# A two-layer hybrid attention trunk on one core: xT in another place, products of zeros at the start, some low parts of weights on GpSimd, and a rearranged compression input

## The chip, the core and the metric

The kernel runs on one core of a Trainium2 chip. The engines are TensorE (PE: matmuls, with the weight loads in their own row, PEld), VectorE (DVE), ScalarE (ACT), GpSimd (POOL) and SyncE (SP, which issues most transfers). The metric is the device time of one execution in microseconds; lower is better. Times of a kernel are the median of several runs; the profile comes from one further execution.

## What is computed

256 tokens of width 1024 pass through two layers. Every layer is `x += Mixer(RMSNorm(x))`, then `x += SqReLU-MLP(RMSNorm(x))`, with a hidden width of 4096, and a last RMSNorm follows. Everything is float32.

- Layer 0: one input projection feeds two groups of heads. Eight heads are "native sparse attention" with three branches (compressed blocks, selected blocks, a sliding window), merged by sigmoid gates; four heads are differential attention. Their outputs are concatenated and go through one output projection.
- Layer 1: block-sparse attention with 16 heads (MoBA), then its MLP.

Of layer 0 the compression branch matters here. Its keys and values are cut into overlapping blocks of 32 tokens, 16 apart, and each block goes through a small network:

```python
tok = jnp.arange(nc)[:, None] * CMP_STRIDE + jnp.arange(CMP_BLOCK)[None, :]
blk = kv[:, :, tok] + pos
hid = jax.nn.gelu(blk.reshape(b, g, nc, CMP_BLOCK * d) @ w1)
return hid @ w2
```

## The kernel before

**Three products for one.** To keep float32 accuracy every matrix product is three matmuls in the fast 32-bit format: both operands are split into a high part and the rest, and `hi*hi`, `hi*lo` and `lo*hi` are added in PSUM (`mm3`, L552 to L554). So every operand needs two parts. ACT copies the high part (L492 for weights, L537 for activations) and DVE subtracts it from the original to get the low part (L495 for weights, L543 for activations).

**Weights** come from HBM as about 200 pieces of 128 x 1024 (512 KB), in the order of use, through five buffers `raw`. `loads` issues the transfers on SP, `splits` makes the two parts, in six slots: three pairs `whi`/`wlo` in the pool `hot`, and three pairs `vhi`/`vlo` in another. `region` gives a piece a slot of one or the other kind, after how its matmuls use it. A `raw` buffer is free again after the low part is made.

**Activations.** `xT` holds the transposed, normalized input (`xTh`, `xTl`), `mT` the output of the heads. Both lie in `hot`. Late parts of `xT` and `mT` also serve as slots for weights, which is why groups such as `xTl<-raw` appear in the profile.

**Start.** Six matmuls of zeros (L519) run while the first data come. Then for both halves of the tokens: sums of squares on ACT and DVE, `rstd` on POOL (L577, L579), the scaling on DVE (L935, with the norm's weights spread over partitions by L919 on PE), eight transposes per half (L615), the split of the transposed tile (`xTh` on ACT, `xTl` on DVE), and the first projection: 24 matmuls of 280 columns (values and gates, unit "vg") per half. The bias table is made by two matmuls (L731), copied (L735), written to HBM (`ud`) and read back in another shape as `B` (2 MB). Unit "k" and the queries follow.

**Heads.** Logits on PE (L778), bias and maximum on DVE (L788, which needs B), exponential on ACT (L792), scaling by `co` and a gate on DVE and POOL (L849), transposes on PE (L812), the split of the transposed probabilities into `Th` and `Tl` (L537, L543), and the product with the values. Differential heads add L1001, L1014 (`KZ`) and L1264 to L1306.

**Compression input.** `got_ckv` (from L954) takes the projected keys and values from PSUM and writes them in the order that the block network needs into `mT`'s low tile: a high copy `kcv` on ACT (L958), four high parts (two on ACT, L972, two on POOL, L976), and four low parts on DVE (L980).

**Order.** Nothing is ordered at run time. A planner (class `Plan`) simulates the engines while the program is built: each step has an engine, or several to choose from, an estimated duration (`t_act`, `t_dve`) and an urgency. Whenever an engine is free, the ready step with the lowest urgency number is written next. On the chip every engine goes through its instructions strictly in that order.

Of the kernel before, what the change touches and what calls it, by code (L numbers as in the profile page):

```python
# [73 lines left out]
def _blocks(ins):  # L74
# [44 lines left out]
    free = set(range(len(out)))  # L119

    def mlp(l):
# [30 lines left out]
def _lay_out(ins):
    f = {k: np.asarray(ins[k]) for k in ins}
    blocks, still = _blocks(ins)
# [9 lines left out]
    for i, nm in enumerate(("ev_lam_q1", "ev_lam_q2", "ev_lam_k1", "ev_lam_k2")):  # L164
# [158 lines left out]
class Slots:  # L323
# [33 lines left out]
    def serve(self):  # L357
        while self.waiting:
            ev, n, only = self.waiting[0]
            got = [i for i in self.items if only is None or only(i)][:n]  # L360
            if len(got) < n:
                return
            self.waiting.pop(0)
            self.items = [i for i in self.items if not any(i is g for g in got)]
# [10 lines left out]
def trunk_kernel(ctx: ExitStack, tc: tile.TileContext, x, w, prm_d, gs, cst_d, eye, out, widths):  # L375
    nc = tc.nc
    widths, still = zip(*widths)
# [178 lines left out]
    def rstd(t, deps):  # L556
# [397 lines left out]
    def got_ckv(b, evs):  # L954

        kcv = acts.tile([128, 2, S], F32R, name="kcv", tag="scr")
# [4 lines left out]
        out = []  # L961
        for g in range(2):
            r = slice(64 * g, 64 * g + 64)
            for s in range(2):
# [653 lines left out]
```

## Time and profile before

| | us |
|---|---|
| median of 3 runs (636.5 to 640.12) | 638.49 |
| the profiled execution | 636.71 |
| its span, first to last instruction | 634.7 |
| PE busy in the span | 619.5 (98%) |
| DVE busy | 399.5 (63%) |
| ACT busy | 354.3 (56%) |
| POOL busy | 92.3 (15%) |

PE counts as busy from a matmul's start to its modelled end, so 98% means that it hardly ever stood idle, not that it ran at its peak. The granted clock was 0.993 of full on average. Some 2 us of the execution lie outside the span. The share of an engine over the whole span says little about the stage in which another engine waits for it, so the rows below are of single stretches.

### The profile page before, as it was taken

Reading aid. Unit: us, or ns where it says so; the run is one execution under the profiler, and the core shown is the slowest. Engines: PE = TensorE matmul, PEld = TensorE weight load, DVE = VectorE, ACT = ScalarE, POOL = GpSimd, SP = SyncE. Lnnn points to the kernel's source line nnn. Section 1 sums busy time; section 2 is a strip of 40 time slices with the busy share of each in tenths; the row PEclk is TensorE's granted clock in tenths of the full one; section 3 lists DMA queues with packets and bytes.
Section 4 is the critical chain, followed back from the end, with each engine's and each line's share of the span. In section 5 each row is a group of like instructions: output and inputs, shape, how many; then the busy total and the mean of one; then the engine's idle time right before and its main releaser. Section 6 shows DMA issues by size and latency. Waiting matters only on the chain.

```text
span 634.7 us, 10488 instructions
## 1 busy us (share of the span) xinstructions
PE 619.5 (98%) x4022; PEld 562.9 (89%) x4022; DVE 399.5 (63%) x722; ACT 354.3 (56%) x647; POOL 92.3 (15%) x111
## 2 busy tenths in 40 slices
PE   8989999899999999999999999999999999999995
PEld 6989899788889899998988999988889999898994
DVE  6899688958743535444576488895753545445264
ACT  5777478746744536343653488975654535345261
POOL 2022011120111211112110011210021211112011
PEclk7999999999999999999999999999999999999999
DMA  8864423514854564645646343562574564645421
GB/s 329 276 243 149 151 101 103 166 65 138 287 175 164 192 207 158 219 154 193 205 166 206 122 140 132 165 202 67 169 269 161 173 223 149 223 162 192 173 68 66
DMA packets 32100, 109.51 MB, mean 173 GB/s; under 512 B 3361, under 2 KB 5681, under 8 KB 32050
## 3 DMA queue, kind: packets, MB, share of 16 engines
q1 hardware_dynamic: 31186, 106.22, 49.8%
q0 software_dynamic: 576, 2.10, 1.1%
q8 instruction: 31, 0.51, 0.3%
q10 hardware_dynamic: 288, 0.52, 0.2%
q14 instruction: 19, 0.16, 0.1%
HBM read 107.76 MB, written 1.07 MB: 171 GB/s over the span
## 4 chain that ended last, share of the span: by engine, by line
PE 86%; DVE 7%; ACT 2%; issue 2%; DMA 2%; POOL 0%; POOLq 0%; DVEq 0%; ACTq 0%
PE ps L554 27%; PE ps L553 26%; PE ps L552 26%; PE ps L778 2%; DMA raw<-in_w_dram 2%; PE ps L812 1%; DVE wlo L495 1%; PE ps L615 1%; DVE vlo L495 1%; DVE mTl L980 1%; DVE Tl L543 1%; ACT P L792 0%; PE ps L519 0%; DVE x L1335 0%; DVE KZ L1014 0%
## 5 line engine op out<-in xcount | busy, mean ns | idle before, releaser
L495 DVE TENSOR_TENSOR vlo<-raw,vhi 128x1024 fp32r<-128x1024 f32 (+1 forms) x96 | 116.6, 1218 | 130.6 <-ACT vhi L492 130.3
L492 ACT ACTIVATE vhi<-raw 128x1024 fp32r<-128x1024 f32 (+1 forms) x96 | 100.3, 1049 | 157.1 <-PE ps L553 144.7
L552 PE MATMUL ps<-xTh,vhi 128*128 128x256 f32 x640 | 182.1, 285 | 0.0
L554 PE MATMUL ps<-xTh,vlo 128*128 128x256 f32 x640 | 181.1, 283 | 0.0
L553 PE MATMUL ps<-xTl,vhi 128*128 128x256 f32 x640 | 181.0, 283 | 0.0
L553 PEld LDWEIGHTS ps<-xTl,vhi 128*128 128x128 f32 x640 | 122.5, 191 | 1.2
L552 PEld LDWEIGHTS ps<-xTh,vhi 128*128 128x128 f32 x640 | 122.5, 191 | 1.2
L554 PEld LDWEIGHTS ps<-xTh,vlo 128*128 128x128 f32 x640 | 122.4, 191 | 0.0
L1398 POOL TENSOR_TENSOR P<-P 128x512 f32<-128x512 f32 x32 | 48.7, 1522 | 308.9 <-ACT P L1395 308.9
L495 DVE TENSOR_TENSOR wlo<-raw,whi 128x1024 fp32r<-128x1024 f32 (+1 forms) x65 | 77.6, 1209 | 9.6 <-ACT whi L492 9.5
L492 ACT ACTIVATE whi<-raw 128x1024 fp32r<-128x1024 f32 (+1 forms) x65 | 66.5, 1040 | 8.9 <-PE ps L554 7.2
L792 ACT ACTIVATE P<-P,nm 128x128 f32<-128x128 f32 x80 | 35.5, 447 | 8.6 <-DVE nm L788 8.5
L552 PE MATMUL ps<-whi,Th 128*128 128x512 f32 x100 | 39.0, 390 | 0.0
L553 PE MATMUL ps<-wlo,Th 128*128 128x512 f32 x100 | 39.0, 390 | 0.0
L554 PE MATMUL ps<-whi,Tl 128*128 128x512 f32 x100 | 38.9, 389 | 0.0
L495 DVE TENSOR_TENSOR mTl<-raw,mTh 128x1024 fp32r<-128x1024 f32 x30 | 35.9, 1219 | 0.1
L492 ACT ACTIVATE mTh<-raw 128x1024 fp32r<-128x1024 f32 x30 | 30.6, 1047 | 1.3 <-PE ps L554 1.3
L1400 DVE TENSOR_TENSOR Tl<-P,Th 128x512 fp32r<-128x512 f32 x22 | 15.2, 693 | 24.9 <-POOL P L1398 24.9
L1395 ACT ACTIVATE P<-ps 128x512 f32<-128x512 f32 x32 | 19.1, 597 | 15.9 <-PE ps L554 12.0
L788 DVE CUSTOM_DVE_ANT_0 P<-ps,B 128x128 f32<-128x128 f32 x80 | 24.5, 351 | 3.7 <-PE ps L778 3.5
L552 PE MATMUL ps<-mTh,Th 128*128 128x512 f32 x68 | 26.6, 391 | 0.0
L553 PE MATMUL ps<-mTl,Th 128*128 128x512 f32 x68 | 26.5, 390 | 0.0
(251 smaller groups left out, 1249.9 us busy)
## 6 DMA issues: line engine op xcount, KB each, us to landing
raw<-in_w_dram SPq DMA_DIRECT2D x192, 512.0 KB, 4.2
B<-ud SPq DMA_DIRECT2D x1, 2048.0 KB, 10.8
gB<-in_gs_dram POOLq DMA_DIRECT2D x4, 512.0 KB, 4.6
x<-in_x_dram SPq DMA_DIRECT2D x2, 512.0 KB, 4.6
raw<-in_w_dram SPq DMA_DIRECT2D x2, 420.0 KB, 5.5
out_dram<-P SPq DMA_DIRECT2D x2, 256.0 KB, 2.1
out_dram<-P ACTq DMA_DIRECT2D x2, 256.0 KB, 2.5
cst<-in_cst_dram SPq DMA_DIRECT2D x1, 372.0 KB
```

The source lines that it names most:

```text
L492: nc.scalar.activation(pc.hi[:, :n], raw[:, :n], AF.Copy)
L495: nc.vector.tensor_tensor(pc.lo[:, :n], raw[:, :n], pc.hi[:, :n].bitcast(F32), OP.subtract)
L543: nc.vector.tensor_tensor(lo, src, hi.bitcast(F32), OP.subtract)
L552: nc.tensor.matmul(out_, ah, bh, start=start, stop=False)
L553: nc.tensor.matmul(out_, ah, bl, start=False, stop=False)
L554: nc.tensor.matmul(out_, al, bh, start=False, stop=stop)
L778: nc.tensor.matmul(ps[:, 128 * qt:128 * qt + nk], q[:, par, ts], k[i][:, par, :nk], start=i == 0, stop=i == 1)
L788: nc.vector.tensor_tensor_reduce(P[:, c], ps[:, c], B[:, h, 0:nk][:, ::-1], -1.0, 3e38, OP.add, OP.min, nm[:, qt:qt + 1])
L792: nc.scalar.activation(P[:, c], P[:, c], AF.Exp, bias=nm[:, qt:qt + 1], scale=-1.0, accum_out=sums[:, qt:qt + 1])
L1395: e = act(t_act(512), lambda: nc.scalar.activation(r, b.t, AF.Relu), got, *deps)
L1398: g = pool(1.225, lambda: nc.gpsimd.tensor_tensor(sq, r, r, OP.mult), e)
L1400: h = dve(t_dve(512), lambda: nc.vector.tensor_tensor(hl, sq, hh.bitcast(F32), OP.subtract), f, g)
```

## The change

- **Places.** All six pairs of weight slots lie in `hot`, in plain order of release; the rule of regions is gone. `xT` moves to the pool `acts`.
- **Products of zeros.** Two further coroutines (`keep_on`) put matmuls of zeros (512 columns, into the bank `ps1`) into PE's order wherever the planner has nothing else for PE, until four pieces of weights have been used. 23 of them come about, besides the six of before.
- **Low parts on GpSimd.** For pieces before number 35 that are at least two ahead of the piece in use, the planner may give the low part to POOL. It does so 14 times.
- **Compression input.** `kcv` holds both parts: ACT makes the high one, DVE the low one, in one 512-wide instruction each, from PSUM. Eight copies then rearrange them into `mT`'s low tile, three on POOL and five on ACT.
- **An estimate.** The planner counts 0.55 in place of 0.93 us for the power in the first norms.

```diff
...
-NEAR = 3
 RAWS, PARTS, NP, URGENT, TAIL, AHEAD = 5, 6, 5, 3, 3, 3
 SECOND, ROOM, LATER = 5, (4, 5), (0, 0.05)
-WARM, WRITE = 6, -1.5
+WARM, WRITE, KEEP, EARLY, SPARE = 6, -1.5, 4, 35, 2
...
-    near = list(zip(tiles(NEAR, [128, 1024], F32R, "whi", hot), tiles(NEAR, [128, 1024], F32R, "wlo", hot)))
+    parts = Slots(plan, list(zip(tiles(PARTS, [128, 1024], F32R, "whi", hot), tiles(PARTS, [128, 1024], F32R, "wlo", hot))))
     tbuf = Slots(plan, list(zip(tiles(2, [128, 512], F32R, "Th", hot), tiles(2, [128, 512], F32R, "Tl", hot))))
-    xT = (hot.tile([128, KT, S], F32R, name="xTh"), hot.tile([128, KT, S], F32R, name="xTl"))
     mT = (hot.tile([128, KT, S], F32R, name="mTh"), hot.tile([128, KT, S], F32R, name="mTl"))
...
-    far = list(zip(tiles(PARTS - NEAR, [128, 1024], F32R, "vhi"), tiles(PARTS - NEAR, [128, 1024], F32R, "vlo")))
-    parts = Slots(plan, [i for p in zip(near, far) for i in p] + near[len(far):] + far[len(near):])
+    xT = (acts.tile([128, KT, S], F32R, name="xTh"), acts.tile([128, KT, S], F32R, name="xTl"))
...
-            got = pc.slots.get(only=region(p) if pc.slots is parts else None)
+            got = pc.slots.get()
...
-            def lo(pc=pc, raw=raw, n=n):
-                nc.vector.tensor_tensor(pc.lo[:, :n], raw[:, :n], pc.hi[:, :n].bitcast(F32), OP.subtract)
+            def lo(eng, pc=pc, raw=raw, n=n):
+                eng.tensor_tensor(pc.lo[:, :n], raw[:, :n], pc.hi[:, :n].bitcast(F32), OP.subtract)
 
             e = act(t_act(n, False), hi, got, loaded[p], u=urgency)
-            f = dve(t_dve(n), lo, e, u=urgency)
+            ways = [(DVE, t_dve(n), lambda lo=lo: lo(nc.vector))]
+            if p < EARLY and p - Piece.current >= SPARE:
+                ways.append((POOL, 0.1 + n / 320, lambda lo=lo: lo(nc.gpsimd)))
+            f = plan.step(ways, [e], urgency)
...
+    def keep_on(z):
+
+        yield zero_e
+        while Piece.uses < KEEP:
+            yield pe(0.23, lambda: nc.tensor.matmul(banks[1].t, z[:, :128], z, start=True, stop=True), u=9)
+
+    for _ in range(2):
+        plan.spawn(keep_on(tbuf.items[1][0]))
...
-        whole = act(t_act(512), lambda: nc.scalar.activation(kcv, ps, AF.Copy), *evs, bank=b)
+        ev = split_out(kcv[:, 0], kcv[:, 1], ps, 512, evs, bank=b)
+        bank_a.put(b, [ev[1]])
...
+        for h in range(2):
+            for g in range(2):
+                for s in range(2):
+                    o, t = slice(64 * s, 64 * s + 64), slice(16 * s, 16 * s + 240)
+                    dst = ckv[o, h, :, g, :, 0:15]
+                    src = kcv[64 * g:64 * g + 64, h, :, t].rearrange("p k (c i) -> p k i c", i=16).bitcast(F32)
+                    ways = [(ACT, 0.575, lambda dst=dst, src=src: nc.scalar.activation(dst, src, AF.Copy))]
+                    if g == s:
+                        ways.append((POOL, 1.25, lambda dst=dst, src=src: nc.gpsimd.tensor_copy(dst, src)))
+                    done.append(plan.step(ways, [ev[h]], 1))
...
```

The line numbers move: L552 to L554 become L547 to L549, L495 becomes L478, L543 L538, L615 L610, L731 L726, L788 L783, L849 L844, L812 L807, L919 L914, L1014 L992; the new matmuls of zeros are L511.

**The order at three places.** First, PE at the start, from its first matmul to the first projection. Before (`gB` is the row of the norm's weights, `ident` the unit matrix of the transposes):

```order
L519 MATMUL ps_117<-Th_81 128x512 x6
L919 MATMUL ps_112<-gB,P_99 128x512
L919 MATMUL ps_113<-gB,P_99 128x512
L615 MATMUL ps_114<-ident,P_95 128x128 x4
L615 MATMUL ps_115<-ident,P_96 128x128 x4
L552 MATMUL ps_110<-whi_74,xTh 128x280
L553 MATMUL ps_110<-wlo_77,xTh 128x280
L554 MATMUL ps_110<-whi_74,xTl 128x280
```

And after the change:

```order
L505 MATMUL ps_117<-Th_87 128x512 x6
L511 MATMUL ps_111<-Th_87 128x512 x5
L914 MATMUL ps_112<-gB,P_103 128x512
L914 MATMUL ps_113<-gB,P_103 128x512
L511 MATMUL ps_111<-Th_87 128x512 x5
L610 MATMUL ps_114<-ident,P_99 128x128 x4
L511 MATMUL ps_111<-Th_87 128x512 x2
L610 MATMUL ps_115<-ident,P_100 128x128 x4
L511 MATMUL ps_111<-Th_87 128x512 x8
L547 MATMUL ps_110<-whi_74,xTh 128x280
L548 MATMUL ps_110<-wlo_80,xTh 128x280
L549 MATMUL ps_110<-whi_74,xTl 128x280
```

Twenty zeros stand ahead of the first projection (L547) now, beside the six of before (L505); three more follow between its parts.

DVE's next rows of the start, before, from the first `xTl` on:

```order
L543 TENSOR_TENSOR xTl<-ps_114,xTh 128x4x128
L543 TENSOR_TENSOR xTl<-ps_115,xTh 128x4x128
L495 TENSOR_TENSOR vlo_103<-raw_91,vhi_100 128x840
L935 SCALAR_TENSOR_TENSOR P_97<-x_119,rs,ps_112 128x512
L935 SCALAR_TENSOR_TENSOR P_98<-x_119,rs,ps_113 128x512
L495 TENSOR_TENSOR wlo_78<-raw_92,whi_75 128x560
L495 TENSOR_TENSOR vlo_104<-raw_93,vhi_101 128x1024
L543 TENSOR_TENSOR xTl<-ps_116,xTh 128x4x128
L543 TENSOR_TENSOR xTl<-ps_117,xTh 128x4x128
```

And after:

```order
L538 TENSOR_TENSOR xTl<-ps_114,xTh 128x4x128
L538 TENSOR_TENSOR xTl<-ps_115,xTh 128x4x128
L478 TENSOR_TENSOR wlo_81<-raw_95,whi_75 128x840
L930 SCALAR_TENSOR_TENSOR P_101<-x_119,rs,ps_112 128x512
L930 SCALAR_TENSOR_TENSOR P_102<-x_119,rs,ps_113 128x512
L478 TENSOR_TENSOR wlo_83<-raw_97,whi_77 128x1024
L478 TENSOR_TENSOR wlo_84<-raw_98,whi_78 128x1024
L538 TENSOR_TENSOR xTl<-ps_116,xTh 128x4x128
L538 TENSOR_TENSOR xTl<-ps_117,xTh 128x4x128
```

Ahead of the second half's `xTl` (from `ps_116` and `ps_117`) stood a split of 560 columns and one of 1024; now it is two of 1024, `wlo_83` and `wlo_84`, both used only after the second half.

Second, the compression input in the middle of the first heads, on DVE, before:

```order
L788 ISA nm 128x1
L495 TENSOR_TENSOR vlo_103<-raw_93,vhi_100 128x1024
L842 RECIPROCAL co<-sums 128x2
L849 TENSOR_SCALAR P_97<-P_97,co,gates 128x128
L980 TENSOR_TENSOR mTl<-ps_110,kcv 64x2x16x15 x4
L543 TENSOR_TENSOR Tl_83<-ps_116,Th_81 128x384
L543 TENSOR_TENSOR Tl_82<-ps_117,Th_80 128x384
```

And after (`kcv` is written from itself because both its parts lie in one tile):

```order
L783 ISA P_103,nm<-ps_115,B 128x128
L783 ISA nm 128x1
L538 TENSOR_TENSOR Tl_89<-ps_116,Th_87 128x384
L538 TENSOR_TENSOR kcv<-ps_110,kcv 128x512
L538 TENSOR_TENSOR Tl_88<-ps_117,Th_86 128x384
L837 RECIPROCAL co<-sums 128x2
L844 TENSOR_SCALAR P_102<-P_102,co,gates 128x128
```

The first `Tl` stands ahead of the one instruction on `kcv`, where it stood behind four on `mTl`. POOL around the same place, before:

```order
L849 TENSOR_SCALAR P_95<-P_95,co,gates 128x256
L849 TENSOR_SCALAR P_96<-P_96,co,gates 128x256
L976 CAST mTl<-kcv 64x2x16x15 x2
L849 TENSOR_SCALAR P_97<-P_97,co,gates 128x256
L849 TENSOR_SCALAR P_98<-P_98,co,gates 128x256
```

And after:

```order
L478 TENSOR_TENSOR wlo_82<-raw_96,whi_76 128x560
L478 TENSOR_TENSOR wlo_81<-raw_96,whi_75 128x1024
L478 TENSOR_TENSOR wlo_84<-raw_94,whi_78 128x1024
L478 TENSOR_TENSOR wlo_80<-raw_97,whi_74 128x1024
L478 TENSOR_TENSOR wlo_81<-raw_96,whi_75 128x1024
L965 CAST mTl<-kcv 64x2x16x15 x3
L844 TENSOR_SCALAR P_103<-P_103,co,gates 128x256
L844 TENSOR_SCALAR P_99<-P_99,co,gates 128x128
L844 TENSOR_SCALAR P_100<-P_100,co,gates 128x256
```

Five splits of weights and the three copies now stand ahead of POOL's first scaling of P (L844). SP between the pieces of weights and B, before:

```order
L423 DMA raw_94<-in_w_dram 128x1024
L423 DMA raw_90<-in_w_dram 128x1024
L423 DMA ud<-P_99 16x383
L423 DMA raw_91<-in_w_dram 128x1024
L423 DMA raw_92<-in_w_dram 128x1024
L423 DMA B<-ud 128x16x256
```

And after:

```order
L409 DMA raw_98<-in_w_dram 128x1024
L409 DMA raw_94<-in_w_dram 128x1024
L409 DMA raw_95<-in_w_dram 128x1024
L409 DMA ud<-P_103 16x383
L409 DMA raw_97<-in_w_dram 128x1024
L409 DMA raw_96<-in_w_dram 128x1024
L409 DMA B<-ud 128x16x256
```

One more piece stands ahead of `ud`, and so of B.

Third, DVE near the end of the differential heads, where the slots of `xT` are filled with weights, before:

```order
L1306 TENSOR_SCALAR od_137<-od_137,dr 128x128
L1001 SCALAR_TENSOR_TENSOR QD_107<-ps_110,QD_107 64x256 x2
L1014 TENSOR_TENSOR KZ<-ps_110,KD_109 64x256
L495 TENSOR_TENSOR xTl<-raw_91,xTh 128x1024
L495 TENSOR_TENSOR xTl<-raw_92,xTh 128x1024
L1014 TENSOR_TENSOR KZ<-ps_110,KD_109 64x256
```

And after:

```order
L1278 COPY od_138<-ps_115 128x256
L979 SCALAR_TENSOR_TENSOR QD_107<-ps_110,QD_107 64x256 x2
L992 TENSOR_TENSOR KZ<-ps_110,KD_109 64x256
L540 SCALAR_TENSOR_TENSOR mTl<-ps_116,sub_128,mTh 128x256
L992 TENSOR_TENSOR KZ<-ps_110,KD_109 64x256
L478 TENSOR_TENSOR xTl<-raw_96,xTh 128x1024
```

Both KZ stand ahead of the one `xTl` that DVE has left; the other is on POOL.

## Rows read from the trace of the kernel before

**Rows 1.** Stretches: length, busy time (count) by engine, PE clock, DMA share, GB/s
```profile
0.00:10.00 10.00, 7.67 (x21) 4.30 (x22) 5.29 (x10) 5.40 (x10) 4.48 (x16) 0.92 0.80 283
10.00:20.00 10.00, 10.00 (x58) 9.56 (x58) 8.94 (x18) 7.88 (x15) 0.01 (x1) 0.74 0.92 349
20.00:40.00 20.00, 20.00 (x170) 20.00 (x169) 16.90 (x46) 13.78 (x34) 0.68 (x2) 1.00 0.93 324
40.00:60.00 20.00, 18.02 (x154) 17.68 (x152) 19.61 (x47) 17.50 (x43) 6.16 (x9) 1.00 0.31 103
...
160.00:360.00 200.00, 200.00 (x1233) 180.35 (x1232) 104.41 (x110) 93.30 (x119) 29.33 (x23) 1.00 0.56 188
```

The busy times stand in the order PE, PEld, DVE, ACT, POOL.

**Rows 2.** PE's waits, 16 to 160 us: waited for, total, times, longest
```profile
PE ps L552 <- DVE KZ L1014: 2.7, 1, 2.7
PE ps L553 <- DVE Tl L543: 2.0, 1, 2.0
PE ps L1216 <- DVE cmpb L1208: 0.6, 1, 0.6
PE ps L812 <- POOL P L849: 0.4, 1, 0.4
```

**Rows 3.** Timeline of DVE: start, us, instruction, count [idle before and releaser]
```profile
16.10 0.69 DVE L543 TENSOR_TENSOR xTl<-ps,xTh 128x512 fp32r<-128x512 f32 x1 [0.79 <-ACT xTh L537]
...
41.75 0.87 DVE L849 TENSOR_SCALAR P<-P,co,gates 128x128 f32<-128x128 f32 x1
42.54 3.99 DVE L980 TENSOR_TENSOR mTl<-ps,kcv 64x480 fp32r<-64x480 f32 x4
46.56 1.02 DVE L543 TENSOR_TENSOR Tl<-ps,Th 128x384 fp32r<-128x384 f32 x2
...
59.82 1.22 DVE L495 TENSOR_TENSOR wlo<-raw,whi 128x1024 fp32r<-128x1024 f32 x1
...
119.64 2.34 DVE L495 TENSOR_TENSOR xTl<-raw,xTh 128x1024 fp32r<-128x1024 f32 x2
```

**Rows 4.** Timeline of POOL
```profile
41.13 2.50 POOL L976 CAST mTl<-kcv 64x480 fp32r<-64x480 f32 x2 [0.56 <-ACT kcv L958]
...
47.83 1.17 POOL L849 TENSOR_SCALAR P<-P,co,gates 128x256 f32<-128x256 f32 x2 [3.54 <-DVE co L842]
...
59.72 1.66 POOL L849 TENSOR_SCALAR P<-P,co,gates 128x256 f32<-128x256 f32 x1 [6.58 <-DVE co L842]
...
164.29 1.04 POOL L1398 TENSOR_TENSOR P<-P 128x512 f32<-128x512 f32 x1 [26.25 <-ACT P L1395]
```

**Rows 5.** Timeline of PE at the start
```profile
4.30 2.31 PE L919 MATMUL ps<-gB,P 1*128 1x512 f32 x4
...
9.70 0.60 PE L554 MATMUL ps<-whi,xTl 128*128 128x280 f32 x1 [0.70 <-DVE xTl L543]
...
15.16 0.41 PE L552 MATMUL ps<-whi,xTh 128*128 128x280 f32 x1
15.40 0.30 PE L553 MATMUL ps<-wlo,xTh 128*128 128x280 f32 x1
15.54 0.30 PE L554 MATMUL ps<-whi,xTl 128*128 128x280 f32 x1
...
19.84 0.28 PE L552 MATMUL ps<-xTh,vhi 128*128 128x256 f32 x1
```

**Rows 6.** Timeline of PE in the output projection, two neighbours of 512 columns
```profile
118.92 0.40 PE L552 MATMUL ps<-whi,mTh 128*128 128x512 f32 x1
119.15 0.39 PE L553 MATMUL ps<-wlo,mTh 128*128 128x512 f32 x1
```

**Rows 7.** The page's groups (count, busy, mean ns, idle before) and a DMA issue
```profile
L495 DVE TENSOR_TENSOR vlo<-raw,vhi 128x1024 fp32r<-128x1024 f32 (+1 forms) x96 | 116.6, 1218 | 130.6 <-ACT vhi L492 130.3
...
L495 DVE TENSOR_TENSOR wlo<-raw,whi 128x1024 fp32r<-128x1024 f32 (+1 forms) x65 | 77.6, 1209 | 9.6 <-ACT whi L492 9.5
...
B<-ud SPq DMA_DIRECT2D x1, 2048.0 KB, 10.8
```

More of the change, by code (lines that the diff above doesn't have):

```diff
@@ L118, in _blocks @@
     out += [r(wo, i) for i in range(4)]
-    free = set(range(len(out)))
     def mlp(l):
@@ L138, in _blocks @@
         out.append(t(odd, span(128 * j, 128 * j + 128), span(1024 + 128 * j, 1152 + 128 * j)))
-    free |= set(range(len(out), len(out) + 4))
     out += [r(f["od_w_out"][0], i) for i in range(4)]
     mlp(1)
-    cut, still = [], []
-    for i, b in enumerate(out):
-        stationary = None if i in free else b.ndim == 4
+    cut = []
+    for b in out:
         b = np.ascontiguousarray(b).reshape(128, -1)
@@ L147, in _blocks @@
         cut += [np.ascontiguousarray(c) for c in np.split(b, k, 1)]
-        still += [stationary] * k
-    return cut, still
+    return cut
 def _lay_out(ins):
     f = {k: np.asarray(ins[k]) for k in ins}
-    blocks, still = _blocks(ins)
+    blocks = _blocks(ins)
     prm = np.zeros((128, P_N), np.float32)
@@ L167, in _lay_out @@
     return {"x": np.ascontiguousarray(f["x"].reshape(S, D)), "w": np.concatenate([b.reshape(-1) for b in blocks]),
-            "prm": prm, "gs": gs, "cst": _constants(), "eye": np.eye(128, dtype=np.float32)}, [(b.shape[1], s) for b, s in zip(blocks, still)]
-NEAR = 3
+            "prm": prm, "gs": gs, "cst": _constants(), "eye": np.eye(128, dtype=np.float32)}, [b.shape[1] for b in blocks]
 RAWS, PARTS, NP, URGENT, TAIL, AHEAD = 5, 6, 5, 3, 3, 3
 SECOND, ROOM, LATER = 5, (4, 5), (0, 0.05)
-WARM, WRITE = 6, -1.5
+WARM, WRITE, KEEP, EARLY, SPARE = 6, -1.5, 4, 35, 2
 ORDER = ["vg", "k", "q0", "c", "q1", "h", "dv", "d0", "d1", "d2", "d3"]
@@ L327, in __init__, with get @@
         self.plan, self.items, self.waiting, self.wanted = plan, list(items), [], []
-    def get(self, n=1, only=None):
+    def get(self, n=1):
         ev = Event()
-        self.waiting.append((ev, n, only))
+        self.waiting.append((ev, n))
         self.serve()
@@ L357, in serve @@
     def serve(self):
[L358 to L364, printed above, removed]
+        while self.waiting and len(self.items) >= self.waiting[0][1]:
+            ev, n = self.waiting.pop(0)
+            got, self.items = self.items[:n], self.items[n:]
             self.plan.fire(ev, "slot", got if n > 1 else got[0])
@@ L472, in loads @@
             plan.when([ev], None, lambda p=p, raw=got.value: plan.fire(loaded[p], SP, raw))
-    def region(p):
-        return None if still[p] is None else lambda it: any(it is f for f in far) == still[p]
     def splits():
@@ L578, in rstd @@
             ms = both
-        return rs, pool(0.93, lambda: nc.gpsimd.tensor_tensor(rs, ms, half[:, 0:1], OP.pow), e, half_e, u=-4)
+        return rs, pool(pow_t, lambda: nc.gpsimd.tensor_tensor(rs, ms, half[:, 0:1], OP.pow), e, half_e, u=-4)
     def rvar(t, deps):
@@ L960, in got_ckv @@
         done = split_out(ckv[:, 0, :, :, :, 15], ckv[:, 1, :, :, :, 15], pos, 64, [prm_e])
[L961 to L964, printed above, removed]
-                o, t = slice(64 * s, 64 * s + 64), slice(16 * s, 16 * s + 240)
-                def part(h, src, r=r, o=o, t=t, g=g):
-                    return ckv[o, h, :, g, :, 0:15], src[r, :, t].rearrange("p k (c i) -> p k i c", i=16)
-                def hi(part=part):
-                    dst, src = part(0, ps)
-                    nc.scalar.activation(dst, src, AF.Copy)
-                def same(part=part):
-                    dst, src = part(0, kcv)
-                    nc.gpsimd.tensor_copy(dst, src.bitcast(F32))
-                def lo(part=part):
-                    (dst, src), (_, high) = part(1, ps), part(1, kcv)
-                    nc.vector.tensor_tensor(dst, src, high.bitcast(F32), OP.subtract)
-                if g == s:
-                    done.append(pool(0.9, same, whole))
-                else:
-                    out.append(act(t_act(480), hi, *evs, bank=b))
-                out.append(dve(t_dve(480), lo, whole, bank=b))
@@ L987, in got_ckv @@
-        bank_a.put(b, [whole, *out])
-        done += out
+        for h in range(2):
[8 more added lines that the diff above has]
+                    done.append(plan.step(ways, [ev[h]], 1))
```

12 lines of the change are left out of this document (5 added, 7 removed).

## The prediction, made before the kernel ran

> **What bounds the kernel now.** First I read the table by stretches [rows 1]: what matters there is how full TensorE (PE) is against the other engines and which clock it was granted. From 160 to 360 us PE is busy 200.00 of 200 us; VectorE (DVE) has 104.41. Nothing that the change does to DVE, ScalarE (ACT) or GpSimd (POOL) can shorten that stretch. The same holds for most of what follows, so I look for gains and losses before 160 us only. [...] And from 20 to 60 us DVE is nearly full, 16.90 and 19.61 of 20 us, so whatever PE needs from DVE there comes when DVE's order allows it.
>
> Then the list of PE's waits, 16 to 160 us [rows 2]: four that matter, 2.7 us for KZ from DVE, 2.0 for Tl from DVE, 0.6 for cmpb from DVE and 0.4 for P from POOL, 5.7 us together. That is all the waiting time an edit could give back after the start; the rest of PE's time is matmuls that the change leaves as they are.
>
> **The wait for Tl.** DVE's timeline [rows 3] shows why it is there: four L980 instructions (low parts of the compression inputs) take 3.99 us from 42.54, and only then, at 46.56, comes Tl, for which PE stands. The change puts the low part of the compression input into one instruction from PSUM, with the first Tl ahead of it in DVE's order, and gives the eight copies to ACT and POOL. A 512-wide instruction of this kind costs 0.69 us (L543 at 16.10 [rows 3]), so DVE drops some 3.3 us and PE's 2.0 us go. Bounds: 0 (Tl late for another reason) to 2.0; I take 2.0, since what was ahead of Tl is gone.
>
> **The wait for KZ.** Two L495 splits of the next xT (2.34 us from 119.64 [rows 3]) stand between two KZ instructions; the second KZ frees the bank that PE waits for. After the change both KZ stand ahead of the one xTl split that DVE keeps, and the other goes to POOL. Bounds 0 to 2.7; I take 2.7.
>
> **The small waits.** POOL's P at 59.72 took 1.66 us, where two of the same width took 1.17 together [rows 4]: a DVE split that began at 59.82 [rows 3] stood in its way. Here fewer DVE splits help, but POOL's own splits now stand in the same queue ahead of L844 (L849 before). Bounds −1.0 (both waits gone) to +1.0 (both doubled); I take −0.4.
>
> **The start.** PE's timeline [rows 5] gives the prices. [...] The price of a zero matmul is 0.23 us at the high clock (512 columns, 118.92 to 119.15 [rows 6]); 23 of them are 5.3 us. They stand ahead of first-pass work in PE's order: five ahead of L914 (which ran at 4.30 [rows 5]), five ahead of the first transposes, two between the transposes, eight ahead of the first projection. Walking through with the durations of the timeline: warm-ups to 4.2, zeros to 5.7, L914 some 1.6 (its 2.31 us were partly at the low clock) to 7.3, zeros to 8.4, transposes and two zeros to 9.8, eight zeros to 11.6; 24 matmuls by 0.14 with eight transposes and three zeros end near 16.2; the 24 of the second token half near 19.4; the bias matmuls 0.4, so the first matmul of unit k stands at about 19.8. Before it stood at 19.84 [rows 5]. But the second half needs xTl from DVE. Its last quarter came at 16.10 [rows 3]. In DVE's order two weight splits of 1.21 us [rows 7] stand ahead of it now, one of them in the place of a 560-wide one, which goes to POOL; that is half a microsecond more, and if POOL's split meets one of the two, another 0.5 to 1. So DVE may hold PE until 20.5. I take 0 for the start. Bounds: −2.8 (all of the clock's gain kept) to +2.5 (all the zeros on the path, less the clock's gain).
>
> [...]
>
> **GpSimd's splits.** Thirteen splits of 1024 and one of 560 leave DVE: 13 x 1.21 + 0.73 = 16.5 us off it (1.209 us each [rows 7]; 0.73 taken in proportion with the fixed part). POOL does 512 elements with two inputs in 1.04 us [rows 4], so 1024 take some 2.1 and all fourteen about 28 us. What they cost beyond that is blocking: L849 of POOL took 1.66 in place of 0.58 us [rows 4], and a DVE L849 that met the POOL copy begun at 41.13 [rows 4] took 0.87 us at 41.75 [rows 3], although it works on half the columns. So a meeting costs the later one 0.5 to 1.1 us. If half of the fourteen meet such a DVE instruction, that is 7 x 0.8 = 5.6 us of lateness, less than what DVE is relieved of, but it comes at other places. POOL's own L844 and the copies of the compression input now wait behind splits, too. I book +1.9 us of new waits on PE, a third of those 5.6; bounds 0 to 5.6.
>
> [...]
>
> **The bias transfer.** B, 2 MB, took 10.8 us to land [rows 7] and gates the first heads' softmax. In the queue of SP one more weight piece now stands ahead of it, in front of ud, and of the two behind ud one has a buffer that a POOL split frees. 512 KB at 324 GB/s [rows 1] are 1.6 us. Half of it had cover (DVE had a split to finish before the first head); I take +0.7, bounds 0 to 1.6.
>
> **The layout, and the plain order of the slots.** Pieces of weights lie in two regions already, whi/wlo and vhi/vlo, and the low splits into both take the same time, 1.209 and 1.218 us [rows 7]. So I book 0 for moving tiles; unseen is xT at its new place, a matmul operand of some 2600 instructions: 1 ns on each would be 2.6 us, in either direction. That goes into the range, with a small chance.
>
> **The sum.** −2.0 −2.7 −0.4 +0 +1.9 +0.7 = −2.5 us. The profiled execution took 636.71 us, its span 634.7; so the same execution would take 634.2. It stands 1.8 below the median of the runs shown, 638.49, and what is compared are medians: 638.5 − 2.5 = 636.0.
>
> **Rivals.** (a) *The start gains.* The clock stays up, the zeros end sooner than in my walk, and DVE has xTl ready when PE arrives: −2.8 more, 633.2. For it speaks that half of the 24 + 24 products ran at the low clock; against it that eight zeros stand right ahead of the first product, and that xTl moves back in time on DVE. 22%.
> (b) *GpSimd holds DVE up* in the full stretch from 20 to 60 us: of each pair of instructions that read two operands from SBUF the later stands still. With 19.61 of 20 us taken, DVE has nowhere to catch up, so the 5.6 us show in full and the Tl wait comes back: 638.5 − 2.7 − 0.4 + 5.6 + 0.7 = 641.7, and up to 643 where the POOL queue delays P as well. It decides as soon as more than half of the splits before 60 us meet a DVE split. For it: the 1.66 and 0.87 us; against: 16.5 us are off DVE. 20%. [...]
> (c) *The zeros do not do what they are for.* They shift the first product to 11.6 us and the clock falls anyway while PE stands for xTl: the 24 products keep 0.23 us each, and the start ends some 2 us later: 638.0. 12%.
> (d) My forecast, 634.5 to 637.5: 46%.
>
> **How the numbers follow.** About 0.5%, 3.2 us, is what a measurement of this kernel can tell from no change; faster means below 635.3, slower above 641.7. Faster: (a) 0.22 and the low third of (d), 0.15, together 0.37. Slower: most of (b), and a small part for xT at its new place, together 0.18. The rest, 0.45, within. The range reaches from 631.5 ((a) with the small waits gone) to 642.5 ((b) but for its end). The predicted time is that of (d).
>
> **What would show it.** In the profile after, PE's waits before 160 us: no wait for Tl near 45 and none for KZ near 119. The clock of the first 20 us at or near full from 5 us on, and the first matmul of unit k within a microsecond of 19.8; earlier by two says (a), later by two with a low clock says (c). POOL's splits near 2.1 us where DVE leaves them alone, and longer ones, or DVE splits above 1.6 us, in 20 to 60 us: many of them with PE's waits behind them say (b). The first softmax instruction of the heads near 36 to 37.5. Wrong as a whole I would be if the stretch from 160 us on changed its length by more than 1 us, since I let it alone.

## The result, and the profile after

The changed kernel takes 649.54 us (median of 4 runs, 648.91 to 651.04), the kernel before 639.31 us beside it; the ratio is 1.0158, with an interval of 1.0118 to 1.0198. The kernel became 10 us slower. The prediction, 636.0 with a range of 631.5 to 642.5, was wrong in sign and in range. The nearest case was rival (b), GpSimd holding DVE up; its price of 641.7 was too low.

The profiled execution took 650.0 us, its span 648.1, against 634.7 before. The first transposes of layer 0's MLP, which start at 157.19 us before, start at 168.00: 10.8 of the 13.4 us are lost before that point, 2.6 after it. Up to 1.7 of the 10.8 are the clock's: in this execution its granted share was 0.50 from 132.43 to 135.84 us, behind a wait of PE of 1.8 us, and in the profiled execution of before it stayed at 1.00 in that stretch.

From the page of the changed kernel: busy time (share of the span) and count per engine, two of the costliest groups (count, busy, mean ns, idle before) and the issue of B.

```profile
PE 626.6 (97%) x4045; PEld 564.8 (87%) x4045; DVE 403.9 (62%) x714; ACT 364.4 (56%) x650; POOL 109.4 (17%) x117
...
L478 DVE TENSOR_TENSOR wlo<-raw,whi 128x1024 fp32r<-128x1024 f32 (+1 forms) x144 | 181.0, 1266 | 74.2 <-ACT whi L475 73.8
...
L478 POOL TENSOR_TENSOR wlo<-raw,whi 128x1024 fp32r<-128x1024 f32 (+1 forms) x13 | 30.9, 2378 | 48.7 <-ACT whi L475 39.7
...
B<-ud SPq DMA_DIRECT2D x1, 2048.0 KB, 12.0
```

DVE was relieved of 14 splits and is busy 4 us longer than before: the time that it stands still inside an instruction counts as busy (12.7 us, below), and seven more scalings of P have come to it (L844, 38 in place of 31). POOL's mean of 2378 ns takes in the one split of 560 columns; those of 1024 took 2.35 to 2.73 us, with a median of 2.39.

The stretches that answer to [rows 1], in the same columns:

```profile
0.00:10.00 10.00, 8.56 (x23) 5.63 (x24) 3.59 (x7) 3.11 (x5) 3.76 (x14) 0.98 0.80 271
10.00:20.00 10.00, 10.00 (x60) 9.08 (x59) 8.34 (x15) 7.28 (x14) 2.44 (x3) 0.85 0.81 302
20.00:40.00 20.00, 19.66 (x162) 18.97 (x160) 14.85 (x28) 14.26 (x28) 8.08 (x4) 1.00 0.88 297
40.00:60.00 20.00, 17.38 (x141) 16.50 (x142) 15.48 (x61) 17.84 (x47) 7.50 (x9) 1.00 0.24 90
```

The granted clock rose from 0.92 and 0.74 to 0.98 and 0.85 in the first two stretches, and DVE has idle time again from 40 to 60 us. Both are what the change can be seen to aim at, and neither shows in the time.

PE's waits, 16 to 175 us, for [rows 2]:

```profile
PE ps L773 <- DVE nm L783: 2.2, 1, 2.2
PE ps L547 <- DVE KZ L992: 1.8, 1, 1.8
PE ps L1194 <- DVE cmpb L1186: 1.7, 1, 1.7
PE ps L807 <- DVE P L1254: 1.1, 2, 0.7
PE ps L548 <- DVE Tl L538: 1.1, 3, 0.5
PE ps L1294 <- DVE od L1284: 0.8, 1, 0.8
```

The 2.0 us for one Tl are gone (four short ones are left, none above 0.5), the wait for cmpb has trebled, KZ is still waited for, and there is a new wait of 2.2 us for the first softmax.

DVE's timeline shows what is behind those for cmpb, P and od:

```profile
23.98 1.91 DVE L1028 TENSOR_SCALAR gates<-gates 128x24 f32<-128x24 f32 x1
...
33.68 2.58 DVE L478 TENSOR_TENSOR wlo<-raw,whi 128x1024 fp32r<-128x1024 f32 x1 [0.17 <-ACT whi L475]
...
82.66 1.29 DVE L1179 TENSOR_TENSOR cmpb<-cmpb,mx 128x256 f32<-128x256 f32 x1
...
120.47 2.18 DVE L1243 TENSOR_TENSOR dco<-dco,lam 128x2 f32<-128x2 f32 x1
...
135.15 3.41 DVE L478 TENSOR_TENSOR wlo<-raw,whi 128x1024 fp32r<-128x1024 f32 x1
```

Beside each of them stands a split on POOL; three of the five:

```profile
23.12 2.73 POOL L478 TENSOR_TENSOR wlo<-raw,whi 128x1024 fp32r<-128x1024 f32 x1 [7.17 <-ACT gates L1024]
...
120.25 2.38 POOL L478 TENSOR_TENSOR wlo<-raw,whi 128x1024 fp32r<-128x1024 f32 x1 [6.01 <-ACT whi L475]
...
134.94 2.54 POOL L478 TENSOR_TENSOR wlo<-raw,whi 128x1024 fp32r<-128x1024 f32 x1 [0.60 <-ACT whi L475]
```

An instruction on two numbers per partition (L1243) takes 2.18 us in place of 0.16, because POOL began its split 0.2 us earlier. Nine of the fourteen splits stop a DVE instruction so, by 0.8 to 2.2 us each, 12.7 us in all (each duration less that of the same instruction undisturbed). Only two of the nine lie between 20 and 60 us.

### The profile page after: what moved, and what is told of

Same layout as the page of the kernel before. It is cut to its first block, busy times and chain, and to the rows that moved or that the text cites. A ratio compares the mean times of both kernels' runs of the same rounds, so it can differ in the third digit from the quotient of the medians.

```text
span 648.1 us, 10579 instructions
## 1 busy us (share of the span) xinstructions
PE 626.6 (97%) x4045; PEld 564.8 (87%) x4045; DVE 403.9 (62%) x714; ACT 364.4 (56%) x650; POOL 109.4 (17%) x117
## 4 chain that ended last, share of the span: by engine, by line
PE 78%; DVE 11%; ACT 5%; issue 3%; DMA 2%; POOL 0%; POOLq 0%; SPq 0%; DVEq 0%; ACTq 0%
PE ps L548 24%; PE ps L549 24%; PE ps L547 24%; DVE wlo L478 3%; DMA B<-ud 2%; DVE P L783 1%; ACT P L787 1%; PE ps L511 1%; PE ps L610 1%; PE ps L773 1%; PE ps L807 1%; DVE Tl L538 1%; ACT mTl L963 1%; DVE P L844 1%; ACT Th L532 1%
## 5 line engine op out<-in xcount | busy, mean ns | idle before, releaser
L478 DVE TENSOR_TENSOR wlo<-raw,whi 128x1024 fp32r<-128x1024 f32 (+1 forms) x144 | 181.0, 1266 | 74.2 <-ACT whi L475 73.8
L475 ACT ACTIVATE whi<-raw 128x1024 fp32r<-128x1024 f32 (+1 forms) x157 | 162.9, 1051 | 95.3 <-PE ps L549 65.8
L547 PE MATMUL ps<-xTh,whi 128*128 128x256 f32 x592 | 169.6, 286 | 0.0
L549 PE MATMUL ps<-xTh,wlo 128*128 128x256 f32 x592 | 166.3, 281 | 0.0
L548 PE MATMUL ps<-xTl,whi 128*128 128x256 f32 x592 | 166.2, 281 | 0.0
L547 PEld LDWEIGHTS ps<-xTh,whi 128*128 128x128 f32 x592 | 111.6, 188 | 0.9 <-issue 0.3
L548 PEld LDWEIGHTS ps<-xTl,whi 128*128 128x128 f32 x592 | 111.7, 189 | 0.6
L549 PEld LDWEIGHTS ps<-xTh,wlo 128*128 128x128 f32 x592 | 111.5, 188 | 0.0
L478 DVE TENSOR_TENSOR mTl<-raw,mTh 128x1024 fp32r<-128x1024 f32 x34 | 41.5, 1224 | 22.9 <-ACT mTh L475 22.9
L549 PE MATMUL ps<-whi,Tl 128*128 128x512 f32 x120 | 46.9, 390 | 0.0
L547 PE MATMUL ps<-whi,Th 128*128 128x512 f32 x120 | 46.7, 390 | 0.0
L478 POOL TENSOR_TENSOR wlo<-raw,whi 128x1024 fp32r<-128x1024 f32 (+1 forms) x13 | 30.9, 2378 | 48.7 <-ACT whi L475 39.7
L547 PE MATMUL ps<-xTh,mTh 128*128 128x256 f32 (+1 forms) x128 | 38.4, 300 | 0.0
L548 PE MATMUL ps<-xTl,mTh 128*128 128x256 f32 (+1 forms) x128 | 38.0, 297 | 0.3 <-DVE xTl L478 0.3
L549 PE MATMUL ps<-xTh,mTl 128*128 128x256 f32 (+1 forms) x128 | 37.8, 295 | 0.0
L547 PE MATMUL ps<-whi,xTh 128*128 128x512 f32 (+1 forms) x88 | 34.0, 387 | 0.1
```

The source lines that it names most:

```text
L475: nc.scalar.activation(pc.hi[:, :n], raw[:, :n], AF.Copy)
L478: eng.tensor_tensor(pc.lo[:, :n], raw[:, :n], pc.hi[:, :n].bitcast(F32), OP.subtract)
L547: nc.tensor.matmul(out_, ah, bh, start=start, stop=False)
L548: nc.tensor.matmul(out_, ah, bl, start=False, stop=False)
L549: nc.tensor.matmul(out_, al, bh, start=False, stop=stop)
```

## Experiments

Each kernel was run beside the kernel before, whose medians lay between 639.0 and 640.8 us; times are medians.

**1. Zeros and GpSimd's splits, each taken away.** The diffs to the changed kernel are one line: `KEEP` 4 to 0 (`a_nozero`), `EARLY` 35 to 0 (`a_nopool`), or both (`a_neither`, shown).

```diff
-WARM, WRITE, KEEP, EARLY, SPARE = 6, -1.5, 4, 35, 2
+WARM, WRITE, KEEP, EARLY, SPARE = 6, -1.5, 0, 0, 2
```

Without zeros, nothing but the zeros leaves PE's order; the other engines' orders are the same (but for two DVE instructions of under 0.2 us that change places in the pair without splits). So the four kernels are a square in which zeros are added or taken away alone. Without splits on GpSimd the planner orders the engines anew, so what the splits cost takes in the order that they bring.

> The changed kernel without its 23 products of zeros (the six of before stay); the order of every other instruction on every engine is the changed kernel's. Theory Z (the zeros stand in the way at the start, and what starts late there comes late again at the bias transfer): the first projection starts 3 us or more earlier than at 14.3 us, the bias matmuls near 19 in place of 22.2, the wait for the first heads' bias shrinks, and the time falls by 3 to 5 us to 644.5 to 646.5. [...] Rival P (GpSimd's splits are all of it): within 1 us of 649.5.

> The changed kernel with all low parts of weights on DVE; zeros, layout and compression input stay. Theory P (a split takes GpSimd 2.4 us, in which DVE instructions stand still, short ones too, and buffers come free late): the time falls by 5 to 8 us, to 641.5 to 644.5, and DVE shows no short instruction of over 1 us. Rival: DVE needed the relief, the 16 us of splits are back on it and the time stays above 648.

> The changed kernel without zeros and without splits on GpSimd: layout, slots in plain order and the compression input are left. Theory Z and P together: nothing of the loss is left, 636 to 639. Rival L (the other order that the plain slots bring, or the places, cost most): 643 or above.

Measured: `a_nozero` 648.14 (ratio to before 1.013, 1.0082 to 1.0178), `a_nopool` 640.68 (1.0007, 0.998 to 1.0034), `a_neither` 640.06 (1.000, 0.9973 to 1.0028). The splits on GpSimd account for the loss: without them the kernel is as fast as before, with them it is 8 to 9 us slower, with or without zeros. That is more than theory P gave. The zeros' share came out at 0.6 and 1.4 us, below theory Z, although in the profiles the bias matmuls stand 3 us later. So the square was run again, with more rounds:

> The changed kernel itself, beside the one without zeros, to set a price on the zeros. In the profiles the bias matmuls stand 3.0 to 3.2 us later with zeros (22.2 against 19.0, 21.7 against 18.6), the medians so far differ by 0.6 and 1.4. Theory Z: 2.5 to 4 us above the one without zeros. Rival (the clock gives most of it back later, or other executions start differently than the profiled ones): 0 to 1.5 us above it.

> The changed kernel without its zeros, every other instruction in the same order. Theory Z: 645 to 647, 2.5 to 4 us under the changed kernel beside it. Rival: less than 1.5 us under it.

> Zeros, but no splits on GpSimd. Theory Z: 2.5 to 4 us above the one with neither. Rival: within 1.5 us of it. In both theories 7 to 10 us under the changed kernel, since the splits are taken away.

> Neither zeros nor splits on GpSimd, the same order on all engines as the one with zeros alone. Theory Z: 2.5 to 4 us under that one. Rival: within 1.5 us of it. In both theories before's time within 1.5 us.

Measured: 650.84 and 647.46 with splits, 641.78 (1.0029, 1.0005 to 1.0054) and 638.02 (0.9981, 0.9956 to 1.0006) without. Zeros: 3.4 and 3.8 us this time; the medians of the four pairs together say that they cost, some 1 to 4 us, no closer. Splits: 9.1 and 9.4 us. `z_neither` lies 2.3 us under before, where at most 1.5 was expected.

The traces of the eight executions say more. The first transposes of layer 0's MLP come 4.1 to 5.0 us later with zeros in all four pairs, where both executions of a pair have the clock low equally long between 20 us and that point. Why the medians show less stays open. With splits they come 7.5 to 8.2 us later. In the pair without zeros, `a_nozero` and `a_neither`, this can be taken apart: 163.33 against 155.71 us, 7.6 us. PE's waits from 16 us to there add up to 8.7 against 3.0 us, and the granted clock of `a_nozero` fell to 0.50 for 3.4 us, worth at most half of that (columns as in [rows 1]):

```profile
127.58:130.99 3.41, 3.41 (x13) 3.02 (x12) 3.27 (x8) 2.63 (x6) 2.64 (x5) 0.50 0.46 136
```

That is 5.7 us of waits and up to 1.7 us of clock. In each of the four traces with splits the clock falls once or twice between 20 us and the MLP (to 0.50 for 3.41 us in the changed kernel and in `a_nozero`, twice as long in `z_all`), in none of the four without. Splits are not needed for it: it falls there in `b_xT`, too, from 122.79 to 133.03 us, which has none.

How the zeros stand in the way is seen in PE's timeline of the changed kernel:

```profile
4.17 2.22 PE L511 MATMUL ps<-Th 128*128 128x512 f32 x5
6.32 1.98 PE L914 MATMUL ps<-gB,P 1*128 1x512 f32 x4
...
11.86 2.61 PE L511 MATMUL ps<-Th 128*128 128x512 f32 x8
14.30 0.29 PE L547 MATMUL ps<-whi,xTh 128*128 128x280 f32 x1
...
22.19 0.52 PE L726 MATMUL ps<-Th,Tl 33*16 33x384 f32 x2
```

and of the one without zeros:

```profile
4.30 2.16 PE L914 MATMUL ps<-gB,P 1*128 1x512 f32 x4
...
7.94 0.47 PE L547 MATMUL ps<-whi,xTh 128*128 128x280 f32 x1
```

The first product starts 6.4 us later. The 24 + 24 products then run at a granted clock of 1.00, 0.13 us apart from 14.30 on, and win half of that back; the bias matmuls stand at 22.19 against 19.02 us, and 21.65 against 18.64 in the pair without splits. The clock was not held, either: from 9.55 to 12.96 us it was at 0.50, and zeros in that stretch stand 0.43 us apart, where those before and behind it stand 0.23. The five from 4.17 to 6.32 us stand 0.43 us apart, too.

The lateness comes back at B. SP's queue in the changed kernel:

```profile
24.07 0.35 SPq L409 DMA_DIRECT2D ud<-P  x1
27.72 0.81 SPq L409 DMA_DIRECT2D raw<-in_w_dram  x2
28.59 0.42 SPq L409 DMA_DIRECT2D B<-ud  x1
```

and without zeros:

```profile
21.14 0.35 SPq L409 DMA_DIRECT2D ud<-P  x1
24.80 0.81 SPq L409 DMA_DIRECT2D raw<-in_w_dram  x2
25.67 0.42 SPq L409 DMA_DIRECT2D B<-ud  x1
```

`ud` is 2.9 us later with zeros, since L726 is; behind it SP stands for 3 us in both kernels, with buffers that a split on POOL (23.12 to 25.85 us) and a stopped DVE free late. B lands at 40.6 us with zeros and at 35.7 without (its transfer took 12.0 against 10.0 us), and the first softmax follows it at 41.1.

**2. The stop by itself.** Nine GpSimd instructions added to the kernel before, for whose result nobody waits, with every other instruction in its old order; DVE is relieved of nothing. In `b_lock` they read two tiles, in `b_write` they only fill one (the line that names `spare` or `idle`, a part of `mT`, is left out).

```diff
...
             f = dve(t_dve(n), lo, e, u=urgency)
+            if p < 20 and p % 2 == 0 and p - Piece.current >= 2:
+                pool(0.0, lambda: nc.gpsimd.tensor_tensor(spare, X[0], X[1], OP.subtract), e, x_e[0], x_e[1], u=9)
```

```diff
...
             f = dve(t_dve(n), lo, e, u=urgency)
+            if p < 20 and p % 2 == 0 and p - Piece.current >= 2:
+                pool(0.0, lambda: nc.gpsimd.memset(idle, 0.0), e, u=9)
```

> The kernel before, every instruction in its old order, and nine GpSimd instructions of 128x1024 besides that read two tiles from SBUF and write a third that is idle then; nothing waits for their result, and DVE is relieved of nothing. Six stand before the first heads, three in them. Theory lock (a GpSimd instruction that reads SBUF stops DVE instructions on SBUF for its whole 2.4 us): DVE instructions of over 1.5 us beside each, POOL's scaling of P late, and 2 to 6 us on the time. Rival queue (the loss comes from low parts and buffers that are ready late, not from the stop): DVE's durations stay, and the time is before's within 1.5 us.

> As the one with nine added GpSimd instructions that read, at the same nine places, but each only fills 128x2048 of an idle tile (about 1.9 us by 0.956 for 1024). Theory lock by reads: DVE instructions with two operands from SBUF keep their 1.22 us beside a fill, and what is lost is less than half of what the reading ones lose. Rival (any GpSimd instruction stops DVE, or it is POOL's queue that delays P): the same loss as with reads.

Measured: reading ones 652.13 (1.0188, 1.0137 to 1.0238), fills 642.61 (1.0018, 0.9987 to 1.005). Nine instructions that do nothing useful cost 11 to 12 us if they read SBUF, about twice the most that theory lock gave, and nothing clear if they only write. With reads, POOL's group and DVE's timeline:

```profile
L502 POOL TENSOR_TENSOR mTh<-x,x 128x1024 fp32r<-128x1024 f32 x9 | 25.0, 2774 | 0.5
```

```profile
11.67 2.94 DVE L497 TENSOR_TENSOR vlo<-raw,vhi 128x840 fp32r<-128x840 f32 x1
...
17.36 3.38 DVE L497 TENSOR_TENSOR vlo<-raw,vhi 128x1024 fp32r<-128x1024 f32 x1
...
24.40 1.92 DVE L1054 TENSOR_SCALAR gates<-gates 128x24 f32<-128x24 f32 x1
```

With fills:

```profile
L502 POOL MEMSET mTh<- 128x2048 f32 x9 | 16.3, 1809 | 0.3
```

```profile
10.12 1.03 DVE L497 TENSOR_TENSOR vlo<-raw,vhi 128x840 fp32r<-128x840 f32 x1
...
13.04 1.22 DVE L497 TENSOR_TENSOR vlo<-raw,vhi 128x1024 fp32r<-128x1024 f32 x1
...
18.00 1.11 DVE L1054 TENSOR_SCALAR gates<-gates 128x24 f32<-128x24 f32 x1
```

Beside a fill, splits keep their 1.03 and 1.22 us; beside a read they take 2.9 and 3.4. The small TENSOR_SCALAR, 0.17 us otherwise, is stopped by both: 1.92 us beside a read, 1.11 beside a fill. So in these two traces the splits, with two inputs from SBUF, stand still beside a GpSimd instruction that reads SBUF and not beside one that only writes it, and this TENSOR_SCALAR beside either. Why, the traces do not say.

PE's two longest waits in `b_lock`, 8 to 175 us; none in that list is for POOL, so POOL's queue is not the way:

```profile
PE ps L735 <- DVE Tl L547: 4.6, 1, 4.6
PE ps L557 <- DVE Tl L547: 3.5, 2, 1.9
```

So the stop alone can be as dear as the whole change, without any relief, extra zeros or another order. It is not the price of the change's own splits: six of the nine reads stand back to back from 11.35 to 28.69 us, where the change has two. Some of it is the clock's, which in this trace is at 0.50 from 26.56 to 33.38 and from 70.93 to 74.34 us, worth up to 5.1. How the change's own loss divides between stops and low parts that POOL finishes late was not measured.

**3. The splits alone, on the kernel before.** The new `lo` and `ways` of the change, nothing else.

> The kernel before with nothing but the choice of GpSimd for low parts of early pieces (the planner takes it 17 times here). Theory P (the splits on GpSimd are what costs): 5 to 10 us above before, with short DVE instructions of over 1 us beside a split. Rival (the splits cost only together with the zeros and the new places): within 2 us of before.

Measured: 653.67 us (1.0195, 1.0158 to 1.0232). Theory P, and above its range: the splits cost 13 us here. There are more of them, 17 in place of 14; eleven stop a DVE instruction, by 18.6 us in all, and in the trace the granted clock is 0.50 for 13.7 us between 20 us and the MLP (3.4 in the changed kernel's). What else the old compression input adds was not separated.

**4. xT's place alone.**

```diff
-    xT = (hot.tile([128, KT, S], F32R, name="xTh"), hot.tile([128, KT, S], F32R, name="xTl"))
...
+    xT = (acts.tile([128, KT, S], F32R, name="xTh"), acts.tile([128, KT, S], F32R, name="xTl"))
```

> The kernel before with xT in the pool acts, every instruction in the same order: the place of xT alone. In the changed kernel matmuls with xT as the stationary operand stand 117 ns apart where they stood 120 before, and those with xT moving 234 where they stood 227. Theory S (that is the place's doing): 1776 x -2 to -3 ns and 216 x +7 ns, so 2 to 4 us less than before, with the same intervals. Rival (it is the weights' place, or the order): the intervals stay 120 and 227 and the time is that of before within 1 us.

Measured: 638.79 us (0.9978, 0.9949 to 1.0007). The intervals are the place's doing: starts of 256-column matmuls with xT stationary stand 117 to 118 ns apart (median, 1920 of them), 120 before; those of 512 columns with xT moving 233 to 235 ns, 227 before. The sum of the two is some 2 us less by the means; in the time it does not stand clear of nothing. In the traces it does: from the MLP's first transposes to the end the four traces in which xT has its new place and the weights their old ones (`b_xT` and experiment 6) take 476.1 to 476.2 us, the six with xT in its old place 477.5 to 478.3.

**5. The two forecast gains, each alone.** The new `got_ckv` in the kernel before (`b_ckv`), and the planner's window for urgent splits:

```diff
-RAWS, PARTS, NP, URGENT, TAIL, AHEAD = 5, 6, 5, 3, 3, 3
+RAWS, PARTS, NP, URGENT, TAIL, AHEAD = 5, 6, 5, 2, 3, 3
```

> The kernel before with the new compression input alone. Theory T (the wait of 2.0 us for Tl near 45 us is worth its length): it is gone, KZ's 2.7 us stay, and the time is 1.5 to 2.5 us under before. Rival (PE's time is bound elsewhere: a wait that goes turns up as another): the wait is gone, others come in the next 20 us, and the time is before's within 1 us.

> The kernel before with the planner's window for urgent splits cut from 3 pieces to 2, which puts both KZ ahead of the xTl splits. Theory K: the wait for KZ falls from 2.7 us to below 1, the clock falls near 125 us in fewer executions, and the time is 2 to 4 us under before. Rival: the wait moves to another operand of the output projection, and the time is before's within 1 us.

Measured: `b_ckv` 636.16 (0.9928, 0.9905 to 0.995), `b_urgent` 639.87 (0.9997, 0.9973 to 1.0021). The compression input alone is worth 3 to 6 us, more than the wait that it removes and than theory T's 1.5 to 2.5. Its waits, 16 to 175 us:

```profile
PE ps L553 <- DVE xTl L495: 0.9, 1, 0.9
PE ps L552 <- DVE KZ L997: 0.9, 1, 0.9
PE ps L812 <- DVE nm L788: 0.8, 1, 0.8
PE ps L1199 <- DVE cmpb L1191: 0.6, 1, 0.6
```

Tl's 2.0 us are down to 0.8 for a first softmax; in the new order that it brings, KZ's 2.7 us are two waits of 0.9. In `b_urgent` KZ's wait is down to 0.2 us, but there are 1.6 us for P from POOL and 2.0 for two Tl: the rival. A reordering that removes a wait moves others, and what it is worth can't be read from that wait alone. The profiles of `b_ckv` and before differ by 0.3 us only, 634.4 against 634.7, because the profiled execution of before, 636.71 us, lies below the medians of before. In `b_xT`, with before's order and a wait for KZ of 2.8 us, the clock is at 0.50 from 122.79 to 133.03 us, which is worth up to 5.1; in `b_ckv` it is from 124.57 to 127.99, up to 1.7; in the profile of before not at all there. So a part of `b_ckv`'s gain can be a clock that falls for a shorter time behind a shorter wait. That is argued, not shown: how often the clock falls was not counted.

**6. What of the change is worth keeping.** First xT's place, the compression input and the window of 2, then the first two without the window:

> The kernel before with xT in its new place, the new compression input, and the planner's window for urgent splits cut from 3 pieces to 2, so that both KZ stand ahead of the xTl splits on DVE; no zeros, no splits on GpSimd. If the two waits of 2.0 and 2.7 us are what can be gained, and xT's place gives 1.5: 633 to 635, that is 4 to 6 us below before, and fewer runs with a low clock near 125 us. Rival (other waits take their place, as in the changed kernel without zeros and splits): 638 to 640.

> xT in its new place, the new compression input and the window of 2 pieces, once more in more rounds. If the terms add up: 0.992 to 0.996 of before. Rival: 0.997 or above.

> The kernel before with the two parts of the change that looked useful by themselves, in the order of the one with the new compression input alone: that compression input (0.9928 of before by itself) and xT's new place (0.9978). If they add up: 0.989 to 0.992 of before, 634 to 635.5. Rival (xT's place gives nothing): 0.992 to 0.995, with intervals of 117 ns for xT stationary and 234 for xT moving.

Measured: 637.07 (0.9958, 0.9924 to 0.9991) and, in more rounds, 637.54 (0.9953, 0.9933 to 0.9973) with the window; 635.53 (0.9945, 0.9921 to 0.9968) without it, every instruction in the order of `b_ckv`. All beat both kernels. In the time, xT's place adds nothing that shows to the compression input's 0.9928; the terms do not add up. The best that the change holds is its compression input.

## Why the prediction was wrong, step by step

- **GpSimd's splits**, the term that failed: booked at +1.9 us with 5.6 as the bound, measured 8 to 9.4 in four pairs. The number of meetings was about right (9 of 14, guessed 7). Three sizes were wrong. A split took 2.39 us, not the 2.1 doubled from the 512-wide row. A meeting cost 1.4 us on average, not 0.8, 12.7 us in all and not 5.6, because the rows of before [rows 3, 4] only had meetings with partners of 1.4 us and less: what a meeting cost here is about what was left of the partner's duration, however short the stopped instruction (2.02 of 2.16 us for the L1243 at 120.47, 2.19 of 2.33 for the split at 135.15). And "a third of those 5.6" on PE had no row behind it: PE's waits alone grew by 5.7 us, and the clock that falls behind them, up to 1.7 us in that pair, had no term at all. The relief of 16.5 us on DVE, on the other side of that sum, bought nothing that shows: with it the splits cost 13 us in `b_pool`, and without it the reads cost 11 to 12 in `b_lock`.
- **The start**: 0 booked, within −2.8 to +2.5; in the traces the bias matmuls came 3.0 and 3.2 us later, outside, and the medians have 0.6 to 3.8. The walk put the first product at 11.6 us; it came at 14.30. It let the zeros stand 0.23 us apart throughout; the trace has five of them ahead of L914 0.43 us apart, and 3.4 us at a clock of 0.50 later: the first transposes were 1.1 us behind the walk, the first product 2.7. The 2.8 us for the clock, in the bounds and in rival (a), no run shows as a gain: the clock was at 0.50 from 8.41 to 15.24 us before and from 9.55 to 12.96 after, half as long, and the bias matmuls came later all the same.
- **B**: +0.7 booked, within 1.6; the wait was 2.2 us with zeros (1.7 in `z_all`). The term took the order of the queue for the whole effect and left out that the start's lateness arrives here again. With splits and without zeros 0.3 to 0.4 us are left.
- **Tl**: −2.0, right for that wait; the edit behind it alone (`b_ckv`) was worth more.
- **KZ**: −2.7, wrong: 1.8 us of wait are left with the splits, 1.1 and another 0.9 for mTh without them.

```profile
PE ps L547 <- DVE KZ L992: 1.1, 1, 1.1
PE ps L547 <- ACT mTh L534: 0.9, 1, 0.9
PE ps L1194 <- DVE cmpb L1186: 0.4, 1, 0.4
```

  These are the waits of `a_neither`. There two xTl stand on DVE between the two KZ again:

```profile
118.32 0.42 DVE L992 TENSOR_TENSOR KZ<-ps,KD 64x256 fp32r<-64x256 f32 x1
...
120.24 1.22 DVE L478 TENSOR_TENSOR xTl<-raw,xTh 128x1024 fp32r<-128x1024 f32 x1
121.49 0.43 DVE L992 TENSOR_TENSOR KZ<-ps,KD 64x256 fp32r<-64x256 f32 x1
```

  In the changed kernel the order on DVE was as read, both KZ ahead of xTl. But QD, KZ and mTl stand there in a chain that starts at 129.01 us, when ACT has made the last KD (L989); by then the projection behind it had been done for over 3 us (its last matmul starts at 125.41), and ACT had been at softmax steps and QD. The second KZ starts at 130.95. The prediction followed DVE's order only, not ACT's.
- **The layout**: 0 booked, with 2.6 us either way; measured nothing clear, with the intervals moving in both directions. But the stretch after 168 us is 2.6 us longer than the one after 157.19 before, where I expected under 1; 1.7 of it is there in `a_neither`, too. The traces separate it: that stretch takes 479.2 to 480.1 us in the changed kernel and all its variants, 476.1 to 476.2 with xT, but not the weights, in the new place, and 477.5 to 478.3 with xT in the old one. So xT's place gives some 1.3 to 2 us, within the 2.6, and 3 to 4 are lost to the slots in `hot` and their plain order, which were booked at 0; the compression input is not it, since it does not lengthen that stretch in `b_ckv` or in `b_xTckv`. This is by difference: no run changed the slots alone.
- **The rivals**: (b) named the mechanism, but not the place: only two of the nine stops lie between 20 and 60 us, and the waits of PE behind stops come later. Its price took the 5.6 us over, so that 641.7 was nearest is in part luck. (c) is half true: the first product came late, at 14.30 us, but the clock was at 1.00 when it came.

## What to carry to other kernels

Before work is given to GpSimd, list which DVE instructions will run beside it: here those with two operands in SBUF, and some `tensor_scalar` too, stood still for nearly all that was left of a GpSimd split, 0.8 to 2.2 us each, so that a planner which knows only durations put 2.4-us blocks in front of 0.2-us instructions on the critical chain. A wait of PE cost twice in the four traces with splits, by its length and by a clock that fell after it, to 0.50 for 3.41 us in that of the changed kernel. Relief of an engine that was not the bound was worth nothing here. Products of zeros stand, in a fixed order, in front of whatever comes early; here they cost more than the clock gave back, some 1 to 4 us.

## What was not expected of the hardware

- The interval of back-to-back matmuls changed with the place of the operand in SBUF: with every instruction in the same order, 120 ns became 117 to 118 for xT stationary (256 columns), and 227 became 233 to 235 for xT moving (512 columns).
- A DVE instruction on two elements per partition took nearly as long as GpSimd's whole instruction beside it: 2.18 us in place of 0.16, beside 2.38.
- The clock differs between executions of one program: the changed kernel was at 0.50 from 9.55 to 12.96 and from 132.43 to 135.84 us in one, and from 7.75 to 11.17, 41.89 to 45.30 and 140.87 to 144.29 in another (`z_all`). With the same order on PE, the low stretch at the start ended at 15.24 us in the profile before and at 13.57 in that of `b_xT`, which shows no stretch at 1.00 ahead of it.
